# Gate groups between the stages of the first mixer, and one scheduling round in place of two

## The chip, the cores and the metric

The kernel runs on one core of a Trainium2 chip. The metric is the device time of one execution in microseconds; of several runs the median is taken.

## What is computed

Two transformer blocks are applied to 256 tokens of width 1024, in float32. The first block is a mixer of three branches (latent attention with 8 heads, a state-space branch with 32 groups, and cross attention to 256 memory tokens) and a gated feed-forward with a causal convolution. The second block has two layers, each a SwiGLU feed-forward, a mixer with three other branches and another SwiGLU feed-forward. For the first mixer the reference reads, cut to what matters here:

```python
h = rmsnorm(x, norm_mix_g)
c_q, c_kv, k_r, u_ssm, x_q, gate_logits = split_combined(h @ w_in)
y_a = mla_branch(c_q, c_kv, k_r, cos, sin, ...) @ w_o_mla
y_b = s5_branch(u_ssm, ...) @ w_o_ssm
y_c = cross_branch(x_q, mem, ...) @ w_o_cross
gates = sigmoid(gate_logits + b_gate).reshape(bsz, l, 3, D_MODEL)
merged = gates[:, :, 0] * y_a + gates[:, :, 1] * y_b + gates[:, :, 2] * y_c
x = x + merged @ w_out
```

## The kernel before

**Products.** Every large product is made of three: each operand is kept as a rounded high part (type fp32r) and the rest. `weights` (L452) loads weights in pieces of 512 KB into one of 5 buffers named raw, and `split` (L541) makes of each 128x512 half a high part wh (a cast on ScalarE) and a low part wl (a subtraction on VectorE). `proj` (L649) gives rows of tokens, in matmuls of up to 512 columns (PSUM tile pr); `proj_T` (L670) gives the transposed result for 256 weight columns in 48 matmuls of 256 columns (PSUM tile pt). Activations are brought into transposed, split form h by `norm_T` (L591): a square with a sum on ScalarE, a power on GpSimd, a scaling on VectorE (tile xs), transposes on TensorE and a split.

**The first mixer** (`mixer1`, L1305) normalises x, makes the latents (cq, ckv), the state-space input u and the cross queries xq, normalises the memory, and then works through the list `ORDER` (L30, loop L1375). Its letters: s0 and s1 are the halves of the state-space branch (`ssm_half`, L1045, with 16 small transfers that regroup u, maps built by `ssm_maps`, L981, of which the tiles xB are transposed into bT; products se of u with bT, a kT product, a scan on VectorE, and the products yb); h0 and h1 are groups of four attention heads (`heads`, L1365, and `mla_heads`, L1234: two projections of the latents, head norms, transposes qt, scores ms, softmax p, outputs mo); k0 and k1 are the two 512-column projections of the normalised memory (tile km); x0 is the cross attention (`cross_attn`, L1153, products cs and co); g0, g1 and g2 are the gate groups of the three branches (`gate_proj`, L816: four calls of `proj_T` and eight tanh on ScalarE into tiles named gate); b0 and b2 multiply the attention and the cross branch's output product with their gate (`branch`, L832). Behind the loop come the state-space GELU and GLU, the third branch and the output product (`merge_out`, L686).

**The rest of the program** (`two_block_kernel`, L1570) is a feed-forward and then two layers of feed-forward, mixer and feed-forward; `norm_x` (L637) stands ahead of each of these seven.

**The order of issue.** No engine instruction is issued while the program above runs. Each is recorded as an operation with an engine, an estimated cost, and the operations that it must follow (`Program.add`, L115). At the end a list scheduler orders all of them, for all engines and for the whole kernel. A round has two passes. `backward` (L154) schedules from the end and takes among the operations that are ready the one that stands latest in the order it was given; the time it gives to an operation is its priority. `forward` (L198) then runs a model of the engines, and takes on each engine the ready operation with the smallest priority for which there is room. Room for a tile is counted against the base order: an operation that stands later than the first one still open gets new tiles only if the base order, followed from there, still finds room for all its own.

```python
if pos[i] > lo:
    v = live[tag]
    ...
    bad = v[lo:pos[i]].max() > self.caps[tag]
```

The caps are 65 work tiles, of which 34 may be split weights, 5 raw buffers, 8 h tiles and 8 PSUM banks. `plan` (L350) begins with the program order as base, and each further round takes the order that the round before gave as its base. `issue` (L358) asks for two rounds and issues the operations in the order that the second gave. Each engine then runs its own instructions in that order and waits where an operand is not there yet.

Of the kernel before, what the change touches and what calls it, by code (L numbers as in the profile page):

```python
# [26 lines left out]
AHEAD = 500  # L27
MARGIN = 0.0
SLOW = 1.0
ORDER = "s0 h0 k0 k1 x0 h1 s1 g0 g1 g2 b0 b2"  # L30
STEPS = [1, 2, 3, 4] + [4 * q for q in range(1, 9)] + [32 * p for p in range(8)]
MAGIC = 12582912.0
TWO_PI = 6.2831850
# [41 lines left out]
class Program:  # L75
# [279 lines left out]
            order = self.forward(prio, order)[1]  # L355
        return order

    def issue(self, tc, rounds=2):  # L358
        with tc.manual_schedule():
            for i in self.plan(rounds):  # L360
                self.ops[i].call()
# [44 lines left out]
class Ctx:  # L406
# [898 lines left out]
    def mixer1(self):  # L1305
# [68 lines left out]
        kvm, y_mla, gates, y_cross = [], {}, {}, None  # L1374
        for step in ORDER.split():  # L1375
            q = int(step[1:])
# [293 lines left out]
```

## Time and profile before

| | us |
|---|---|
| median of 3 runs | 1574.74 |
| lowest and highest run | 1571.79, 1578.25 |
| the profiled execution | 1573.03 |
| its span, first to last instruction | 1571.3 |
| TensorE busy with matmuls | 1553.6 |
| TensorE busy with weight loads | 1430.9 |
| VectorE busy | 1025.7 |
| ScalarE busy | 840.1 |
| GpSimd busy | 101.7 |

A matmul's busy time runs from its start to a modelled end, and matmuls overlap in the pipeline; so a mean duration is longer than the distance between two starts, and a short wait can hide in the overlap. PE is TensorE's matmuls, PEld its weight loads, DVE VectorE, ACT ScalarE, POOL GpSimd and SP the engine whose queue issues the transfers. A wait is named by the instruction that waited and by what released it. L398 and L497 are helpers that issue nearly everything, so instructions are told apart by the names of their tiles.

### The profile page before, as it was taken

Reading aid. Unit: us, or ns where it says so; the run is one execution under the profiler, and the core shown is the slowest. Engines: PE = TensorE matmul, PEld = TensorE weight load, DVE = VectorE, ACT = ScalarE, POOL = GpSimd, SP = SyncE. Lnnn points to the kernel's source line nnn. Section 1 sums busy time; section 2 is a strip of 40 time slices with the busy share of each in tenths; the row PEclk is TensorE's granted clock in tenths of the full one; section 3 lists DMA queues with packets and bytes.
Section 4 is the critical chain, followed back from the end, with each engine's and each line's share of the span. In section 5 each row is a group of like instructions: output and inputs, shape, how many; then the busy total and the mean of one; then the engine's idle time right before and its main releaser. Section 6 shows DMA issues by size and latency. Waiting matters only on the chain.

```text
span 1571.3 us, 28497 instructions
## 1 busy us (share of the span) xinstructions
PE 1553.6 (99%) x11145; PEld 1430.9 (91%) x11145; DVE 1025.7 (65%) x1820; ACT 840.1 (53%) x1759; POOL 101.7 (6%) x204
## 2 busy tenths in 40 slices
PE   9999999999999999999999999999999999999998
PEld 7889999899989999889998999899998899989997
DVE  7896897787676545756657554665457656575543
ACT  8766665765555544555446444455345554464442
POOL 5114600000000000000000000000000000000000
PEclk9999999999999999999999999999999999999999
DMA  8556164566556656555647665466664556476650
GB/s 284 174 151 178 44 211 138 191 217 212 185 175 221 208 195 210 158 158 164 212 138 235 200 208 193 148 221 203 207 209 148 167 162 198 146 233 209 203 186 28
DMA packets 214230, 287.79 MB, mean 183 GB/s; under 512 B 13904, under 2 KB 170192, under 8 KB 214096
## 3 DMA queue, kind: packets, MB, share of 16 engines
q1 hardware_dynamic: 213952, 285.71, 57.0%
q8 instruction: 88, 1.44, 0.4%
q14 instruction: 46, 0.38, 0.1%
q10 hardware_dynamic: 144, 0.26, 0.0%
HBM read 284.36 MB, written 1.05 MB: 182 GB/s over the span
## 4 chain that ended last, share of the span: by engine, by line
PE 89%; DVE 4%; ACT 2%; DMA 2%; issue 1%; POOL 0%; POOLq 0%; DVEq 0%; ACTq 0%
PE pt L497 50%; PE acc L497 21%; PE pr L497 7%; PE up L497 4%; PE tr L522 2%; ACT wh L398 1%; DVE wl L398 1%; DMA raw<-in_w_ffn_dram 1%; DVE xs L398 1%; DMA raw<-in_w_in_dram 1%; DVE x L398 1%; PE se L497 1%; PE ms L497 0%; PE warm L629 0%; PE yb L497 0%
## 5 line engine op out<-in xcount | busy, mean ns | idle before, releaser
L398 DVE TENSOR_TENSOR wl<-raw,wh 128x512 fp32r<-128x512 f32 x1045 | 657.2, 686 | 193.9 <-ACT wh L398 184.0
L497 PE MATMUL pt<-h,wh 128*128 128x256 f32 x4224 | 736.1, 277 | 0.0
L398 ACT CAST wh<-raw 128x512 fp32r<-128x512 f32 x1045 | 578.3, 618 | 147.2 <-DMA raw<-in_w_in_dram 43.3
L497 PEld LDWEIGHTS pt<-h,wh 128*128 128x128 f32 x4224 | 642.4, 188 | 2.8 <-issue 0.2
L497 PE MATMUL pt<-h,wl 128*128 128x256 f32 x2112 | 584.1, 277 | 0.0
L497 PEld LDWEIGHTS pt<-h,wl 128*128 128x128 f32 x2112 | 397.0, 188 | 0.7 <-issue 0.5
L497 PE MATMUL acc<-wh,gh 128*128 128x512 f32 x440 | 170.6, 388 | 0.0
L497 PE MATMUL acc<-wh,gl 128*128 128x512 f32 x440 | 170.6, 388 | 0.0
L497 PE MATMUL acc<-wl,gh 128*128 128x512 f32 x440 | 170.4, 387 | 0.0
L497 PE MATMUL pr<-wh,h 128*128 128x512 f32 (+2 forms) x480 | 130.8, 355 | 2.4 <-DVE h L398 2.3
L398 ACT CAST gh<-sg 128x512 fp32r<-128x512 f32 x47 | 29.2, 621 | 147.5 <-DVE sg L398 147.5
L497 PE MATMUL up<-wh,h 128*128 128x512 f32 x320 | 100.8, 390 | 0.1
L497 PEld LDWEIGHTS pr<-wh,h 128*128 128x128 f32 x480 | 84.5, 188 | 16.0 <-DVE h L398 2.5
L497 PEld LDWEIGHTS acc<-wh,gl 128*128 128x128 f32 x440 | 82.6, 188 | 17.0
L497 PEld LDWEIGHTS acc<-wl,gh 128*128 128x128 f32 x440 | 82.5, 188 | 16.0
L497 PEld LDWEIGHTS acc<-wh,gh 128*128 128x128 f32 x440 | 82.6, 188 | 15.9
L398 DVE TENSOR_TENSOR sg<-sg,pt 128x512 f32<-128x512 f32 x36 | 24.8, 688 | 110.1 <-PE pt L497 110.1
L398 ACT ACTIVATE sg<-pt 128x512 f32<-128x512 f32 x36 | 21.5, 598 | 130.4 <-PE pt L497 130.4
L497 PE MATMUL pr<-wl,h 128*128 128x512 f32 (+2 forms) x240 | 85.0, 354 | 0.0
L398 POOL TENSOR_TENSOR rs<-s,mhalf 128x1 f32<-128x1 f32 x20 | 16.4, 820 | 961.8 <-DVE s L398 961.8
L497 PEld LDWEIGHTS up<-wh,h 128*128 128x128 f32 x320 | 59.7, 188 | 12.5 <-ACT h L398 0.6
L398 ACT ACTIVATE junk<-x 128x512 f32<-128x512 f32 x36 | 22.7, 631 | 79.1 <-DVE x L398 76.2
(352 smaller groups left out, 1639.8 us busy)
## 6 DMA issues: line engine op xcount, KB each, us to landing
raw<-in_w_ffn_dram SPq DMA_DIRECT2D x264, 512.0 KB, 5.0
raw<-in_w_in_dram SPq DMA_DIRECT2D x124, 512.0 KB, 5.0
raw<-in_w_up_dram SPq DMA_DIRECT2D x44, 512.0 KB, 4.8
raw<-in_w_out_dram SPq DMA_DIRECT2D x24, 512.0 KB, 4.8
raw<-in_w_down_dram SPq DMA_DIRECT2D x22, 512.0 KB, 4.5
raw<-in_w_mem_kv_dram SPq DMA_DIRECT2D x8, 512.0 KB, 4.5
raw<-in_w_branch_ret_dram SPq DMA_DIRECT2D x8, 512.0 KB, 3.5
raw<-in_w_o_mla_dram SPq DMA_DIRECT2D x4, 512.0 KB, 3.5
```

Source lines behind the costliest of these rows:

```text
L398: self.prog.add(self.name, lambda: getattr(self.eng, op)(**kw), self.cost(op, kw), list(aps.values()), writes, "fast" if self.name == "dve ...
L497: self.prog.add("pe", lambda: self.nc.tensor.matmul(ps, lhsT=lhsT, rhs=rhs, start=start, stop=stop), ns, [lhsT, rhs], [ps])
L522: self.prog.add("pe", lambda: self.nc.tensor.transpose(out, src, ident), 109, [src, ident], [out])
```

## The change

Two lines. The gate groups g0 and g1 move forward in the list, the memory projections, the cross attention and their order against h1 and s1 change with it, and the scheduler makes one round, so that the program order is the base for the whole kernel.

```diff
-ORDER = "s0 h0 k0 k1 x0 h1 s1 g0 g1 g2 b0 b2"
+ORDER = "s0 g0 h0 h1 g1 s1 k0 k1 x0 g2 b0 b2"
...
-    def issue(self, tc, rounds=2):
+    def issue(self, tc, rounds=1):
         with tc.manual_schedule():
             for i in self.plan(rounds):
                 self.ops[i].call()
```

## Rows read from the trace of the kernel before

**Rows 1.** The page, busy time of each engine over the whole span.

```profile
span 1571.3 us, 28497 instructions
PE 1553.6 (99%) x11145; PEld 1430.9 (91%) x11145; DVE 1025.7 (65%) x1820; ACT 840.1 (53%) x1759; POOL 101.7 (6%) x204
```

**Rows 2.** Busy time by stretch: length, engines' busy us and counts, clock, DMA.

```profile
0.00:256.00 256.00, 246.24 (x2084) 225.99 (x2085) 213.74 (x437) 177.84 (x471) 78.73 (x164) 0.99 0.56 171
256.00:1571.00 1315.00, 1307.32 (x9063) 1204.86 (x9061) 811.98 (x1384) 662.27 (x1288) 23.00 (x40) 1.00 0.58 186
```

**Rows 3.** TensorE's waits, 0 to 256 us: total us, times, longest.

```profile
PE pr L497 <- DVE h L398: 2.3, 1, 2.3
PE tr L522 <- DVE ckv L398: 1.4, 1, 1.4
PE tr L522 <- DVE p L398: 1.3, 1, 1.3
...
PE yb L497 <- DVE sg L398: 0.9, 1, 0.9
PE se L497 <- ACT bT L398: 0.8, 1, 0.8
PE mo L497 <- ACT p L398: 0.7, 1, 0.7
...
PE tr L522 <- POOL x L392: 0.3, 1, 0.3
PE tr L522 <- DVE xB L398: 0.3, 1, 0.3
```

**Rows 4.** TensorE's waits, 256 us to the end.

```profile
PE tr L522 <- DVE xs L398: 0.7, 4, 0.2
PE tr L522 <- DVE sg L398: 0.3, 1, 0.3
```

**Rows 5.** Busy time by stretch around the slow stretch, in the columns of rows 2.

```profile
157.00:162.00 5.00, 3.64 (x29) 2.86 (x28) 4.18 (x14) 3.83 (x10) 3.43 (x10) 1.00 0.32 105
162.00:170.00 8.00, 8.00 (x61) 7.41 (x62) 6.43 (x14) 3.45 (x7) 4.85 (x9) 0.59 0.22 66
```

**Rows 6.** Instructions of the gate tiles: ns shortest/median/longest, first and last start.

```profile
L398 ACT ACTIVATE gate<-pt,hbg x24: 457/470/505, 106.9 to 219.0; 128x256 f32<-128x256 f32 x24
```

**Rows 7.** TensorE in order of time, s0's and s1's transposes: start, us, idle before.

```profile
93.56 0.60 PE L522 MATMUL tr<-par,xB 128*128 128x128 f32 x4
93.91 0.48 PE L497 MATMUL pt<-h,wh 128*128 128x256 f32 x2
...
158.20 1.14 PE L522 MATMUL tr<-par,xB 128*128 128x128 f32 x8
159.60 0.63 PE L522 MATMUL tr<-par,xB 128*128 128x128 f32 x4 [0.26 <-POOL x L392]
160.48 0.63 PE L522 MATMUL tr<-par,xB 128*128 128x128 f32 x4 [0.25 <-DVE xB L398]
161.96 5.73 PE L497 MATMUL se<-u,bT 128*128 128x64 f32 x32 [0.85 <-ACT bT L398]
```

**Rows 8.** The chain that ended last, state-space products of s0: start, us.

```profile
97.06 1.75 PE se L497 x16
```

**Rows 9.** What SP's queue waited for: total us, times, longest.

```profile
SPq L449 <- DVE wl L398: 1169.7, 494, 11.6
```

**Rows 10.** Transfers by name: count, KB each, median us to landing.

```profile
raw<-in_w_in_dram SPq DMA_DIRECT2D x124, 512.0 KB, 5.0
```

**Rows 11.** TensorE in order of time around 463 us, the up products between left out.

```profile
463.07 0.49 PE L497 MATMUL up<-wh,h 128*128 128x512 f32 x1
...
467.38 1.06 PE L522 MATMUL tr<-par,xs 128*128 128x128 f32 x8 [0.18 <-DVE xs L398]
```

**Rows 12.** Busy time by stretch, 256-column and mostly 512-column products, columns of rows 2.

```profile
720.00:808.00 88.00, 88.00 (x768) 88.00 (x768) 53.71 (x89) 43.72 (x82) 0.00 (x0) 1.00 0.63 200
...
564.00:575.00 11.00, 11.00 (x51) 9.13 (x50) 9.38 (x16) 7.07 (x13) 1.40 (x6) 1.00 0.52 172
```

## The prediction

> **What bounds the kernel now.** I read the page's busy times first, then the busy time on either side of the end of the first mixer, then what TensorE waited for on either side, and last the places where it waited. TensorE has matmuls in flight for 1553.6 us of a span of 1571.3 us [rows 1], so 17.7 us of idle time is all that shows. Of it, 256.00 - 246.24 = 9.76 us lie in the first 256 us, the first mixer, and 1315.00 - 1307.32 = 7.68 us in everything behind it [rows 2]. The lists of waits say what that time is. In the mixer they are 2.3 us for the normalised memory on its way to the key and value product, 1.4 us for a latent, 1.3 and 0.7 us for softmax rows, 0.9 us for the state-space products, 1.4 us (0.8 + 0.3 + 0.3) for the second half's matrices [rows 3]; the rest of the 9.8 us, 1.8 us, is the start's, ahead of any stage that moves. Behind the mixer TensorE waits for other engines 1.0 us in all [rows 4]; the rest there is sequencer time and the store at the end, in which no product is left to run. The clock adds one loss that idle time doesn't show: it was at 2.4 GHz nearly throughout, but the stretch 162 to 170 us has a mean grant of 0.59, that is, most of it at 1.2 GHz; just before it, from 157 to 162 us, TensorE was busy 3.64 of 5.00 us [rows 5].
>
> So an order of instructions is the whole subject. The work stays what it is: no matmul, cast, subtraction or transfer is added or dropped, the sum of the durations is the same, and what can move is some 10 us of waits and one slow stretch in the mixer, and whatever a different schedule does to the 1315 us behind it.
>
> **The change, part by part.** The profiled execution took 1573.03 us, 1.7 us over its span and 1.7 us under the median of 1574.74 us; the sum is made on 1573.0 and 1.7 us is added for the median.
>
> *The order of the stages in the program.* Groups g0 and g1 (4 products of 48 matmuls each, 8 transfers of 512 KB, 16 casts and 16 subtractions a group) come forward, g0 to just behind the state-space half s0, g1 to just ahead of s1; k0, k1 and x0 (8 transfers, 16 casts and subtractions, the cross attention) go back behind s1, and the two head groups h0 and h1 stand together. The program order isn't the order of issue: already now a gate's tanh runs at 106.9 us and the last at 219.0 us, though the groups stand at the end of the list [rows 6], so gate products already serve as filler. What I cost is what the named waits become.
>
> (a) k0 moves behind both head groups and s1, so the normalised memory is wanted tens of us later than now, when TensorE stood 2.3 us for it [rows 3]. Taken: -2.3 us. Bounds: -2.3, or 0 where another late tile takes its place (the nearest row is the 1.4 us for a latent).
>
> (b) The latents are made ahead of the list, and VectorE, which makes them, is as full as before (213.74 of 256 us [rows 2]). The 1.4 us stay: 0.
>
> (c) s0 stays first, with gate products behind it before (by the schedule) and after (by the program): its 0.9 us stay. Bounds: -0.9 to +0.9.
>
> (d) The softmax waits, 1.3 + 0.7 us, came from one head group. Two of them stand together now, each with the same chain from scores over exponentials to transposes; gate products on both sides are filler, but in the profile they were there too. Taken: 0. Bounds: -2.0 to +2.0.
>
> (e) s1's preparation. In the profile 16 transposes of its matrices run from 158.20 us with nothing between them and gaps of 0.26, 0.25 and 0.85 us [rows 7]; s0's same transposes have gate products between them, and no wait. With g1 written just ahead of s1, s0 is the nearer row. Taken: -1.4 us. Bounds: -1.4 to +1.4.
>
> (f) The slow stretch follows (e). By the chain 32 state products took 5.73 us in it, where 16 took 1.75 us for s0 [rows 7, 8]: 5.73 - 2 x 1.75 = 2.2 us more, and that is the least, since a head group's and the kT products stand in the stretch too. By the grant, 8.00 us at 0.59 did what 4.7 us would at 2.4 GHz: 3.3 us [rows 5]. Taken: -3.3 us, for the whole stretch, since (e) goes with it. Bounds: -3.3, or +3.3 where the changed order makes one such stretch more than now.
>
> What moves with the stages on other queues: SP's transfers wait for freed buffers, 494 times for the subtraction that frees one [rows 9], so k0's and g0's weights only change places in that queue, and TensorE never waited for a transfer by name [rows 3, 4]. The second half's 16 small transfers pass ahead of k0's weights; its memsets and the head groups' rotations change places on GpSimd, which is idle 256.00 - 78.73 = 177.27 us of the mixer [rows 2]. Cost 0; if that cover went, a late 512 KB weight would cost part of its 5.0 us from issue to landing [rows 10].
>
> *One round in place of two.* The second round takes the first one's order as its base: for ties, for the priorities and for which tiles may be taken early. Without it the base is the program order, over the whole kernel. No row shows such a schedule. From below: behind the mixer only 1.0 us of waits is there to be won [rows 4]. From above: there are seven normalisations ahead of a feed-forward or mixer, each covered by products of the other token tile. At the one near 463 us, up products begin at 463.07 us and cover the second tile until its transposes at 467.38 us; without cover that is 4.3 us [rows 11], 30 us for seven. I take +2.8 us, 0.4 us each: the row nearest is the wait of 0.18 us there, which says that cover is just enough now and little is needed to miss. As a bound I keep half the cover, +15 us.
>
> The sum: -2.3 - 1.4 - 3.3 + 2.8 = -4.2 us, 1568.8 us, with 1.7 us **1570.5 us**, a quarter of a per cent under the median. The ends: -2.3 - 0.9 - 2.0 - 1.4 - 3.3 - 1.0 = -10.9 us, 1563.8 us; and 0.9 + 2.0 + 1.4 + 3.3 + 15 = +22.6 us, 1597.3 us.
>
> **How much room is there?** The rows say some 10 us of waits and 3.3 us of clock. The Trainium skill, "Perfetto Trace Analysis", section "Identifying the Most-Contended Engine", holds matmul busy time for a bad measure and judges headroom by the busy share of weight loads. By that share, 91%, 140.4 us would be open [rows 1], and a better order could win far more than my sum. The trace bears it out little: where 256-column products run back to back weight loads are busy 88.00 of 88.00 us, but where mostly 512-column ones do, TensorE has no gap and the loads are busy 9.13 of 11.00 us [rows 12]. The share falls with the shape there, not with a stall.
>
> **The rivals.** A difference under 0.5% (7.9 us) is about what a measurement of this kernel can't tell from no change.
>
> *All of it goes.* Gate products between the stages cover every chain: the waits of the mixer but the 1.8 us at its start (9.8 - 1.8 = 8.0 us) and the 3.3 us of clock, and the single round costs nothing: 1573.0 - 11.3 + 1.7 = 1563.4 us. For it: six of the eight waits of the mixer's stages stand in s0, s1 and the head groups, which the gate groups now flank. Against: gate products were at hand during most of them, and TensorE waited because an instruction placed ahead of them was late. By the Trainium skill's measure up to 140.4 us could go, to 1434 us; the rows above leave that 0.01 of this rival's chance.
>
> *The order issued hardly differs.* Gates were spread from 106.9 to 219.0 us already [rows 6], and the scheduler may undo the rearrangement: 1574.7 us, give or take 3 us. Against it: k0's place is bound to its program position through the tie-break.
>
> *The single round loses cover behind the mixer.* With the program order as base, the next stage's weights and tiles are taken later, because the program order's own peaks hold the room. Its place is the seven normalisations. At 2.5 us each it costs 17.5 us; with -7.0 us from the mixer the time is 1573.0 + 10.5 + 1.7 = 1585.2 us. It decides from (7.9 + 7.0) / 7 = 2.1 us each. For it: the cover is tight (0.18 us of wait). Against: the cover follows from the program order itself, in which the second tile's last products stand behind the first tile's.
>
> **How the numbers follow.** The forecast has 0.32, the unmoved order 0.15; both are within 0.5%, so 0.47. The full gain has 0.28, all of it faster by over 0.5%. The lost cover, with its like in the mixer, has 0.25, slower by over 0.5%. The range reaches from 1562 us, the full gain and the ends of its scatter, to 1587 us, just past the lost cover; about 0.1 is left out on each side. The middle cases alone lie between 1567 and 1582 us.
>
> **What would show it.** Right: no wait of the key and value product for the memory; the second half's transposes with gate products between them; the grant 1.00 through the mixer; the merge of the mixer starting 6 to 8 us sooner; behind it the same stretches as now, longer by under 0.5 us at each normalisation. Wrong: waits for softmax rows or state products that total over 10 us, a second slow stretch, or waits of 2 us and more ahead of the up products.

## The result, and the profile after

| | before | after |
|---|---|---|
| median, us | 1574.13 | 1583.2 |
| lowest and highest run | 1571.07, 1578.25 | 1581.15, 1585.06 |
| the profiled execution | 1573.03 | 1585.06 |
| its span | 1571.3 | 1583.3 |
| its mean granted clock | 0.997 | 0.993 |

The changed kernel is slower: the ratio over five runs of each is 1.0062, with a 95% interval of 1.0045 to 1.0079, that is 9.1 us. It lies in the predicted range and on the other side of the forecast. The profiled execution of the kernel after is the slowest of its five, that of the kernel before is a little under its median; so the two profiles differ by more, 12.0 us, than the medians. The page of the kernel after, where [rows 1] stood before:

```profile
span 1583.3 us, 28503 instructions
PE 1560.4 (99%) x11145; PEld 1436.5 (91%) x11145; DVE 1024.6 (65%) x1820; ACT 840.6 (53%) x1759; POOL 96.7 (6%) x204
```

The work is the same, x11145 matmuls, and TensorE is busy 6.8 us longer with it, which a wait cannot do and a slower clock can. Next the busy time by stretch, cut where the mixer's output product (tile acc) has just begun, at 260.29 us; the columns are those of [rows 2]. The kernel before, cut at the same product (255.67 us), follows:

```profile
0.00:260.29 260.29, 250.27 (x2082) 229.07 (x2083) 209.41 (x432) 176.51 (x467) 73.88 (x164) 0.97 0.53 164
260.29:1583.30 1323.01, 1310.12 (x9064) 1207.47 (x9063) 815.15 (x1389) 664.07 (x1293) 22.78 (x40) 1.00 0.58 185
```

```profile
0.00:255.67 255.67, 245.91 (x2082) 225.74 (x2083) 213.41 (x437) 177.76 (x471) 78.73 (x164) 0.99 0.56 171
255.67:1571.30 1315.63, 1307.65 (x9064) 1205.12 (x9063) 812.31 (x1384) 662.34 (x1289) 23.00 (x40) 1.00 0.58 185
```

So 4.6 us were lost in the mixer, after as many matmuls (x2082), and 7.4 us behind it. Idle time in the mixer is 260.29 - 250.27 = 10.0 us, where it was 9.8 us; the grant fell from 0.99 to 0.97. Behind it idle time rose from 8.0 to 12.9 us.

TensorE's waits after the change, first those up to 275 us ([rows 3] before), in total us, times, longest:

```profile
PE tr L522 <- DVE xB L398: 4.3, 1, 4.3
PE warm L629 <- DVE warm L392: 1.3, 1, 1.3
PE kT L497 <- POOL cT L392: 1.2, 1, 1.2
PE pr L497 <- ACT h L398: 1.1, 1, 1.1
PE pr L497 <- DVE wl L398: 1.1, 2, 0.8
```

Then those behind it ([rows 4] before):

```profile
PE up L497 <- ACT h L398: 4.8, 5, 2.3
PE ss L497 <- ACT qks L398: 1.5, 1, 1.5
```

Every wait of the mixer's stages that the prediction named has gone: the memory, the latent, the softmax rows, the products yb and se. Others stand in their place, one of 4.3 us for tile xB among them; and behind the mixer up products wait for the split activations h. The clock is read from four short stretches, in the columns of [rows 5]:

```profile
11.00:15.00 4.00, 3.69 (x15) 3.33 (x15) 4.00 (x10) 4.00 (x11) 1.05 (x3) 0.57 1.10 355
79.00:83.00 4.00, 3.10 (x16) 2.95 (x17) 3.79 (x11) 1.17 (x2) 1.48 (x6) 0.57 0.03 10
181.00:192.00 11.00, 10.34 (x59) 7.99 (x60) 6.96 (x14) 2.55 (x7) 7.92 (x14) 0.53 0.01 3
840.00:844.00 4.00, 4.00 (x13) 3.11 (x12) 3.42 (x8) 2.55 (x6) 0.94 (x1) 0.57 0.44 125
```

TensorE ran at 1.2 GHz for some 3.4 us from 11 us, 3.4 us from 79.3 us, 10.2 us from 181.7 us and 3.4 us from 840.5 us, 20.4 us together, where the kernel before had some 6.8 us [rows 5]; since 1.2 GHz is half of 2.4, the slow time of a stretch is twice its length times what the grant lacks of 1, as in 2 x 4.00 x (1 - 0.57) = 3.4 us. The 13.6 us more at half the clock cost 6.8 us, which is what TensorE's busy time grew by. Each of the four stretches follows a wait of TensorE: 1.13 us for h that end at 9.50 us, the 4.30 us for xB, 2.30 us for h that end at 839.34 us, and ahead of the longest stretch this one:

```profile
181.66 0.65 PE L497 MATMUL kT<-cT,x 128*32 128x128 f32 x8 [1.18 <-POOL cT L392]
```

That leaves three theories, with the letters used below. **C**, SP's queue: under the new list the second half's small transfers are issued much too early and hold up the weights of the head group behind them. **G**, the clock: chains of transposes and short products now stand where the clock falls. **A**, the single round: cover is lost behind the mixer. A rival to C and G is that the new list is no worse in itself, and that the single round alone costs the time.

### The profile page after: what moved, and what is told of

It reads as the page before. It is cut to its first block, busy times and chain, and to the rows that moved or that the text cites. A ratio compares the mean times of both kernels' runs of the same rounds, so it can differ in the third digit from the quotient of the medians.

```text
span 1583.3 us, 28503 instructions
## 1 busy us (share of the span) xinstructions
PE 1560.4 (99%) x11145; PEld 1436.5 (91%) x11145; DVE 1024.6 (65%) x1820; ACT 840.6 (53%) x1759; POOL 96.7 (6%) x204
## 4 chain that ended last, share of the span: by engine, by line
PE 92%; DVE 3%; DMA 2%; issue 1%; ACT 1%; SPq 0%; POOL 0%; POOLq 0%; DVEq 0%; ACTq 0%
PE pt L497 49%; PE acc L497 20%; PE pr L497 9%; PE up L497 7%; PE tr L522 2%; DVE wl L398 1%; DMA raw<-in_w_in_dram 1%; DMA raw<-in_w_ffn_dram 1%; PE ms L497 0%; SPq L449 0%; PE yb L497 0%; DVE x L398 0%; ACT wh L398 0%; PE glu L497 0%; DMA raw<-in_w_up_dram 0%
```

## The experiments

**The list and the round apart.** e1 keeps the old list and makes one round; e2 takes the new list and makes two.

```diff
(e1, on the kernel before)
-    def issue(self, tc, rounds=2):
+    def issue(self, tc, rounds=1):
(e2, on the kernel after)
-    def issue(self, tc, rounds=1):
+    def issue(self, tc, rounds=2):
```

> The old list with one round. Theory A (the single round is what costs behind the mixer, since it issues the first token tile's transposes and its cast of h later): behind the mixer the same 6 to 8 us as in the changed kernel appear, with waits of up products for the cast of h of some 4 to 5 us in all; the mixer is within 3 us of the kernel before; the time is 1578 to 1583 us. Rival B (the list is what costs, in the mixer and through what it shifts): 1572 to 1576 us, waits of up products under 1 us.

> The new list with two rounds. Theory A: behind the mixer as in the kernel before, no wait of up products over 0.5 us; what is left of the loss is the mixer's, at most 5 us: 1572 to 1579 us. Rival B: the mixer loses its 4 to 5 us and some of the waits behind it stay: 1579 to 1584 us.

Measured, in medians (with the ratio to the kernel before, and its interval):

| | two rounds | one round |
|---|---|---|
| old list | 1574.3 | 1592.9 (1.0124, 1.0108 to 1.0140) |
| new list | 1581.2 (1.0051, 1.0038 to 1.0065) | 1583.2 (1.0062, 1.0045 to 1.0079) |

The new list alone costs 7 us, so the rival falls. e1 lies above both of its expected ranges. A single round costs 18.6 us with the old list and 2.0 us with the new one (these two intervals overlap, so the 2.0 us may be nothing): the two edits don't add. TensorE's waits of e1 in its first 275 us say where:

```profile
PE se L497 <- ACT bT L398: 4.5, 1, 4.5
PE pr L497 <- ACT h L398: 4.4, 2, 3.3
PE yb L497 <- DVE sg L398: 2.9, 1, 2.9
```

These are chains of the mixer, and e1's output product begins only at 272.5 us. TensorE's idle time up to there is 272.50 - 254.03 = 18.5 us, where the kernel before had 9.8 us, and 10.1 us behind it (8.0 us). The clock of e1's runs was 0.9915 on average, that of the kernel before beside them 0.9971; (0.9971 - 0.9915) x 1593 = 8.9 us is an estimate of what that cost, about half of the loss. The gates' tanh run from 130.4 us on in e1, from 106.9 us in the kernel before [rows 6] and from 71.8 us in the kernel after. So it may be that with the old list as base the gate products come too late to cover the chains, and that the new list makes the single round bearable there; no run shows it. e2 has nearly the wait of after:

```profile
PE tr L522 <- DVE xB L398: 4.1, 1, 4.1
PE ms L497 <- ACT qkT L398: 2.2, 1, 2.2
```

So the wait for xB belongs to the list and not to the round.

**What the wait for xB hangs on.** It is followed back in the kernel after. TensorE in order of time (start, us, idle before and its releaser in brackets):

```profile
75.21 0.38 PE L497 MATMUL pr<-wl,ckvh 128*128 128x512 f32 x1
...
79.89 1.09 PE L522 MATMUL tr<-par,xB 128*128 128x128 f32 x4 [4.30 <-DVE xB L398]
```

VectorE, which makes xB, had been idle earlier, and ScalarE ahead of it; first ScalarE's, then VectorE's row:

```profile
67.12 0.51 ACT L398 CAST wh<-raw 128x384 fp32r<-128x384 f32 x1 [1.25 <-DMA raw<-in_w_q_b_dram]
```

```profile
67.67 0.56 DVE L398 TENSOR_TENSOR wl<-raw,wh 128x384 fp32r<-128x384 f32 x1 [3.97 <-ACT wh L398]
```

The transfer that came last is a head group's weights. SP issued it here, in order of time:

```profile
51.26 3.66 SPq L449 DMA_DIRECT2D u<-uT  x5
55.02 0.53 SPq L449 DMA_DIRECT2D raw<-in_w_in_dram  x1
55.61 1.89 SPq L449 DMA_DIRECT2D u<-uT  x2
57.60 0.53 SPq L449 DMA_DIRECT2D raw<-in_w_q_b_dram  x1
58.17 6.21 SPq L449 DMA_DIRECT2D u<-uT  x9
64.48 0.53 SPq L449 DMA_DIRECT2D raw<-in_w_q_b_dram  x1
```

The 16 small transfers u<-uT are the second half's, not wanted until some 175 us; before the change they were issued from 85 to 97 us. Together they fill SP for 3.66 + 1.89 + 6.21 = 11.8 us, with the head group's pieces of w_q_b between and behind them. The piece issued at 64.48 us, 192 KB, is the one for which ScalarE and then VectorE stood.

e3 takes these 16 transfers out of the issued order and puts them back behind the head groups' last weights. Only SP's order changes.

```diff
-            for i in self.plan(rounds):
+            for i in self.late(self.plan(rounds)):
                 self.ops[i].call()
...
+    def late(self, order):
+        move = set([i for i, op in enumerate(self.ops) if op.kind == "move"][16:])
+        order = [i for i in order if i not in move]
+        at = order.index(self.behind) + 1
+        return order[:at] + sorted(move) + order[at:]
```

> The changed kernel with the 16 small transfers of the second state-space half issued behind the head groups' weights, where SP is free, and every other engine's order untouched. Theory C (those transfers, 0.6 us each on SP, hold up the weights of the head groups, VectorE waits for these, and the first half's matrices and TensorE's 4.3 us wait follow): the wait at 80 us falls under 1.5 us, and the slow stretch that followed it goes; the time is 4 to 6 us under the changed kernel, 1577 to 1580 us. Rival D (VectorE is full there anyway, and its order sets the wait): 0 to 1 us under it, 1582 to 1584 us.

e4 undoes one step that theory A suspected behind the mixer. At 839.34 us of the kernel after, up products wait 2.30 us for h; the transposes of the first token tile stand behind all output products, and ScalarE's cast of h stands behind a cast of weights that was itself late:

```profile
838.18 0.62 ACT L398 CAST wh<-raw 128x512 fp32r<-128x512 f32 x1 [1.96 <-DMA raw<-in_w_ffn_dram]
838.71 0.58 ACT L398 CAST h<-tr 128x512 fp32r<-128x512 f32 x1
```

At the same place the kernel before has the first tile's transposes between output products, and its cast of h ahead of that cast of wh. e4 moves them so at all seven normalisations, in TensorE's and ScalarE's order:

```diff
+    def hoisted(self, order):
+        for b, trs, cast in self.hoist:
+            move = [*trs, cast]
+            pe = [i for i in order if self.ops[i].eng == "pe"]
+            before = pe[pe.index(trs[0]) - (7, 4)[b]]
...
+            order = order[:at] + move + order[at:]
```

> The changed kernel with the first token tile's transposes at each of the seven normalisations of x issued 7 and 4 products earlier, and their casts of h right behind them, as in the kernel before; all else untouched. Theory A: the waits of up products for the cast of h (4.8 us) fall under 1 us and the slow stretch near 840 us goes: 4 to 6 us under the changed kernel, 1577 to 1580 us. Rival E (the weights are what is late, and TensorE then waits for the low part of a weight instead): under 1.5 us won, 1581.5 to 1584 us.

Measured: e3 1578.01 us (1.0031, 1.0019 to 1.0043), 5.2 us under the kernel after; e4 1585.8 us (1.0084, 1.0067 to 1.0100), 2.6 us over it, with intervals that overlap, and outside both of its expected ranges. TensorE's wait for xB in e3, whose lines stand 6 further down, and then SP's order in it:

```profile
PE tr L528 <- DVE xB L404: 2.2, 1, 2.2
```

```profile
67.79 0.37 SPq L455 DMA_DIRECT2D raw<-in_w_kv_b_dram  x1
68.21 10.18 SPq L455 DMA_DIRECT2D u<-uT  x16
```

With nothing changed but the place of 16 transfers in one queue, the time falls and the wait halves: C holds for the time. Two things that it expected didn't come: the wait was to fall under 1.5 us, and the slow stretch behind it was to go. VectorE begins with xB at 74.85 us rather than 78.90 us; but it is busy 9.72 of the 10.00 us from 70 to 80 us, so the 2.2 us that are left look like its own order. And in e3's profile the slow stretch behind the wait is longer, not shorter (below); that run, 1581.89 us, is one of the slowest of e3's twelve. e4's waits behind the mixer:

```profile
PE tr L533 <- DVE xs L409: 5.9, 9, 1.1
PE ss L508 <- ACT qks L409: 1.6, 1, 1.6
```

The up products' wait has gone and the transposes' wait for xs, which the kernel after doesn't have there, is 5.9 us at nine places: the wait has moved one instruction on. So the place of those transposes and casts by itself isn't what the single round costs; that reading of A fell, and A itself stayed open.

**C without the round, and the clock.** e5 is e2 with e3's edit. For G, three kernels put extra products among the transposes of both state-space halves: ahead of the first and third of each group of four stands one product of 256 columns in bf16, whose result the transposes overwrite; 16 products in all. e6 does so on the kernel before, e7 on e3.

```diff
-        bT = [[self.copied(self.transposes(m), "bT") for m in part] for part in xin]
+        bT = [[self.copied(self.busy_transposes(m), "bT") for m in part] for part in xin]
...
+    def busy_transposes(self, src):
+        i = len(self.prog.ops)
+        ps = self.transposes(src)
+        for op in self.prog.ops[i:i + 4:2]:
+            op.call = lambda call=op.call: (self.fill(ps), call())
+        return ps
+
+    def fill(self, ps):
+        rhs = self.ident.bitcast(BF16)
+        self.nc.tensor.matmul(ps[:, 256:512], lhsT=self.identb, rhs=rhs, start=True, stop=True)
```

For A, e8 keeps the single round's times for the operations of the first mixer and takes two rounds' times for all the rest:

```diff
+    def merged(self):
...
+        for r in range(2):
...
+            starts.append(start)
+        n = self.border
+        shift = max(starts[0][:n]) - max(starts[1][:n])
+        key = [starts[0][i] if i < n else starts[1][i] + shift for i in range(len(self.ops))]
```

> The new list with two rounds, and the 16 small transfers of the second state-space half issued behind the head groups' weights, all else untouched. Theory C (these transfers on SP are the list's cost): 3 to 5 us under the same kernel without it, 1576 to 1578 us, and the 4.1 us wait for the first half's matrices falls under 2 us. Rival F (the list costs through the head groups' softmax and projections, whose waits sum to 6 us there): within 1.5 us of 1581 us.

> The kernel before, with 8 extra bf16 products of 256 columns among the transposes of each state-space half's matrices, into a bank that those transposes overwrite; 16 products in all, about 0.1 us each. Theory G (the clock falls because TensorE does little but transposes with gaps there): the slow stretch of 6.8 us goes or shortens, the mean granted clock of the runs rises by 0.001 to 0.002, and the time is 0 to 3 us under the kernel before, 1571 to 1574 us. Rival H (the clock falls for another reason, or at a random time): the products only cost, 0.5 to 2 us more, 1574.5 to 1576.5 us, clock as before.

> The changed kernel with the second half's transfers late, as before, and with the same 16 extra products. Theory G: the slow stretches after 77 us and after 182 us shorten (13.7 and 6.8 us in the profile without the products), the mean clock rises by 0.002 to 0.004, 2 to 5 us under the same kernel without them, 1573 to 1576 us. Rival H: 1578 to 1580 us.

> The changed kernel, but the operations behind the first mixer in the order that a second round gives them; the mixer keeps the order of the first round. Theory A (the single round costs 6 us behind the mixer): the waits of up products and of the stick-breaking scores (6.3 us) fall under 2 us, 4 to 6 us under the changed kernel, 1577 to 1579.5 us. Rival I (the loss behind the mixer comes from where the mixer ends and what is loaded ahead then, not from the order behind it): 1581.5 to 1584 us.

Measured:

| | median, us | ratio to before | mean clock of its runs |
|---|---|---|---|
| before | 1573.58 | | 0.997 |
| e5 | 1574.99 | 1.0011 (0.9999 to 1.0022) | 0.998 |
| e6 | 1572.43 | 0.9990 (0.9979 to 1.0000) | 0.998 |
| e7 | 1574.23 | 1.0005 (0.9996 to 1.0014) | 0.998 |
| e8 | 1578.79 | 1.0034 (1.0020 to 1.0048) | 0.994 |

e5 is 6.2 us under e2: C is worth as much with two rounds as with one, and it is nearly all that the new list costs there. The mean clock rose with it, from 0.9948 to 0.9976, which by (0.9976 - 0.9948) x 1581 = 4.4 us is most of the 6.2 us; so what the late weights cost came for a good part as clock, and C and G are not separate there.

e7 is 3.8 us under e3, with 16 products more. Two stretches of e3 by clock, and then the same two of e7, in the columns of [rows 5]:

```profile
77.00:91.00 14.00, 13.86 (x89) 13.01 (x88) 9.17 (x26) 9.13 (x34) 6.87 (x15) 0.52 0.28 81
181.00:192.00 11.00, 9.82 (x68) 7.75 (x68) 8.06 (x16) 2.48 (x8) 7.97 (x15) 0.69 0.01 2
```

```profile
77.00:91.00 14.00, 13.60 (x133) 12.57 (x132) 13.20 (x31) 11.54 (x40) 6.58 (x15) 1.00 0.29 83
181.00:192.00 11.00, 10.79 (x95) 9.74 (x96) 8.31 (x18) 6.60 (x24) 3.94 (x6) 1.00 0.01 4
```

The grant is 1.00 where it was 0.52 and 0.69, and in the same 14 us 133 matmuls run in place of 89. e3's profile shows one of its slowest runs, but over all runs the mean clock is 0.9947 in e3 and 0.9984 in e7, and their intervals are apart: G holds for this list. The wait for xB ahead of the first stretch is 2.2 us in e7 as in e3, so the wait alone doesn't decide; that for cT ahead of the second one fell from 1.2 to 0.5 us. What the products do is shorten the slow stretch: e9 below has the same mixer, wait and products as e7, and in its profile the clock does fall behind the wait, but for 3.4 us (a grant of 0.57 from 77 to 81 us, 1.00 from 181 to 192 us), where e3 has 13.7 us. On the kernel before the same edit shows little; e6's slow stretch is still there, with a grant of 0.66:

```profile
162.00:170.00 8.00, 7.34 (x60) 6.62 (x60) 7.12 (x17) 3.66 (x8) 5.66 (x10) 0.66 0.21 68
```

Its 1.2 us of gain have an interval that touches 1.0000: not settled.

e8 is 4.4 us under the kernel after, and in its profile 1316.0 us follow the output product's start, as in the kernel before (1315.6 us; 1323.0 us in the kernel after), with 8.0 us of idle time where the kernel after has 12.9 us. The profiles differ there by more than 4.4 us, since that of e8 is of its quickest run and that of the kernel after of its slowest. TensorE's only wait behind the mixer is

```profile
PE tr L545 <- DVE xs L421: 1.3, 5, 0.4
```

where after has 4.8 + 1.5 = 6.3 us. So the single round's loss under the new list lies behind the mixer, as A says, and two rounds' order there takes it back. Which of that order's many differences does it isn't shown; the one that was tried, in e4, is not it.

**All three together.** e9 is e8 with e3's and e7's edits; e10 is e5 with e7's.

> The changed kernel with all three remedies: the second half's transfers late, the 16 extra products among the transposes, and the operations behind the mixer in the order of a second round. If the three losses are separate (theories C, G and A), their gains add up: 1583.2 - 5 - 4 - 4.5, about 1569 to 1571 us, 3 to 4 us under the kernel before, with the mixer's output product starting near 252 us as without the second round. Rival J (they share one loss, so that one remedy hides another): 1573 to 1576 us.

> The new list with two rounds, the second half's transfers late and the 16 extra products: what the list is worth without the single round. Theory: as the kernel with late transfers alone (1575.0 us) less what the clock gives back, at most 2 us: 1572.5 to 1575 us, so the list with two rounds is no better than the old list with the extra products (1572.4 us). Rival J: 1570 us or less.

e9 took 1570.51 us (0.9979, 0.9971 to 0.9988), 3.1 us under the kernel before; e10 1574.44 us (1.0004, 0.9993 to 1.0016). The three steps before were 5.2 us (e3), 3.8 us (e7, on top of e3) and 4.4 us (e8), 13.4 us in all, which would give 1569.8 us; they nearly add. e9's waits in the mixer, and its first 252.8 us by the columns of [rows 2]:

```profile
PE tr L551 <- DVE xB L427: 2.2, 1, 2.2
PE warm L669 <- DVE warm L421: 1.3, 1, 1.3
PE pr L526 <- ACT h L427: 1.2, 1, 1.2
```

```profile
0.00:252.80 252.80, 246.44 (x2098) 225.69 (x2099) 208.97 (x433) 176.41 (x468) 74.70 (x164) 0.99 0.54 170
```

Its output product begins at 252.8 us, 2.9 us sooner than in the kernel before, with 16 matmuls more and idle time of 252.80 - 246.44 = 6.4 us where that had 9.8 us [rows 2]. With two rounds for the mixer too, e10 gets to 255.7 us, no sooner than the kernel before. The fair comparison for the 16 products is e6, the kernel before with the same ones: there the output product begins at 256.2 us, with 9.7 us of idle time. So in these profiles the new list does cover the mixer's chains better, and with the first round's order only; in the change as it was made this stood under three losses. In time e9 is 1.9 us under e6, with intervals that overlap (0.9971 to 0.9988 and 0.9979 to 1.0000): that the change gains anything without its losses isn't settled.

## Why the prediction was wrong

The forecast, 1570.5 us, is e9's time by chance: e9 moves 16 transfers, adds 16 products and takes two rounds behind the mixer, none of which the forecast had. Two of the three signs of being wrong that the prediction named came: a second slow stretch, and a wait of 2 us and more ahead of the up products. Point by point:

- **(a), (d), (e), the named waits: gone, as forecast or better.** No wait of [rows 3] that the prediction dealt with is left, also those for the latent and the softmax rows that (b) and (d) kept at 0. The forecast's error is what took their place: idle time in the mixer is 10.0 us, where 9.8 - 3.7 = 6.1 us was forecast. For (e) the number is luck: 14 of the second half's 16 transposes stand in a row at 176.85 us, with no gate products between them, and a wait came behind them, the 1.18 us for cT.
- **"What moves with the stages on other queues: cost 0" failed.** The prediction named the 16 small transfers that "pass ahead of k0's weights" and the price of a late 512 KB weight, and then argued from TensorE's waits that no transfer was late. In the new list they stand ahead of a head group's weights, and each takes SP's sequencer about 0.59 us. By e3 that cost 5.2 us, by e5 6.2 us, the clock that went with it included. TensorE's waits still name no transfer; they name xB, some steps down the chain. The Trainium skill, "DMA: Bandwidth & Descriptors", section "Issuing engines are not separate DMA queues", holds that what an issuing engine's sequencer spends on a transfer is usually small beside the transfer. The rows show a case that this doesn't cover: one such transfer of 16 KB takes SP some 0.6 us, with 1.8 us from issue to landing (medians), 9 of them in a row took SP 6.21 us, and what counted was the 192 KB of weights behind them. The same step priced GpSimd by its idle time, 177.27 us; but it is GpSimd's last clearing of cT, up to 181.6 us, for which TensorE stood 1.18 us ahead of the longest slow stretch. No run moves that clearing, so its price stays open.
- **(f), the clock, had the wrong sign.** It was taken at -3.3 us because (e) would go. (e)'s waits did go, and the slow stretch stayed: from 181.7 us, in the second half's products, right behind the wait for cT that took their place. Waits go ahead of all four slow stretches, but a wait alone doesn't set how long one lasts: behind the same 2.2 us for xB the clock stayed low for 13.7 us in e3, for 3.4 us in e9 and not at all in e7, the last two with 16 products more. What else decides stays open. The bound "one such stretch more" was too small too: three more came, at 11, 79 and 840 us, the last one behind the 2.30 us wait of the up products. The mean clock was 0.9938 in the five runs of the kernel after and 0.9969 in the 30 runs of the kernel before beside e5 to e8; (1 - 0.9938) x 1583 - (1 - 0.9969) x 1574 = 4.9 us is an estimate of the cost, about half of the 9.1 us, and the fill of e7 takes back 3.8 us. With -3.3 us in the sum, this term is the furthest off.
- **The single round: the right sign and place, under-sized.** Taken at +2.8 us, 0.4 us for each of seven normalisations; e8 measures 4.4 us behind the mixer. The mechanism was near: TensorE's waits of 4.8 us fall on the up products, at five of the seven normalisations. What the prediction had not seen is that the round's cost depends on the list, 18.6 us with the old one and 2.0 us or nothing with the new.
- **The rival with the lost cover** came out near in time, 1585.2 us against 1583.2, and half right: its place is where part of the loss was, but at 0.6 us (4.4 / 7) a normalisation, far from the 2.1 us from which it was to decide. The rest came from C and G, for which there was no rival on the slow side.

Put together, by the two profiles: the forecast had -3.7 us of waits in the mixer, +2.8 us of waits behind it and -3.3 us of clock. TensorE's idle time shows +0.2 us in the mixer and +4.9 us behind it (12.9 - 8.0), and the slow stretches +6.8 us: 11.9 us, against 12.0 us between the two spans. The medians are 9.1 us apart, with some 4.9 us for the clock. The gains of e3, e7 and e8 are another cut through the same loss and can't be put into this sum one by one: e3 and e5 gave back waits and clock together.

## What to carry to other kernels

When stages change places, write down for each queue, SP's too, which transfers now stand ahead of which, and when each is wanted; a string of cheap transfers that is wanted late should be issued late, and its delay shows not as a wait for a transfer but as an idle helper engine some steps up the chain. Waits that vanish are replaced by the next ones in line, so count a gain only once the instruction behind is known to be ready. Read the granted clock of each short stretch before and after an edit: a schedule can lose as much there as in waits, with TensorE busy throughout.

## What the runs showed of the hardware

The granted clock wasn't steady from run to run of the same kernel: of all runs of the kernel before beside these experiments the quickest took 1569.63 us at a mean grant of 0.999 and the longest 1578.77 us at 0.995; by (0.999 - 0.995) x 1574 = 6.3 us, an estimate, most of its scatter of 9.1 us is the clock's. The clock fell behind a wait of 2.2 us and stayed at 1.2 GHz for some 13 us in a stretch that itself had no gap to speak of but held transposes and narrow products (e3, 77 to 91 us: TensorE busy 13.86 of 14.00 us, grant 0.52). Behind a wait as long, with products that compute nothing among the transposes (16 in all), it stayed at 2.4 GHz in the profile of e7 and fell for 3.4 us in that of e9, so that adding work made the kernel 3.8 us faster (e7 against e3). The stretch at 11 us came in the profile of after and not in that of before (its grant there was 1.00). e3, whose order differs from that of after only by transfers issued much later, has a grant of 1.00 there, and a wait for h of 0.46 us in place of 1.13 us; so the order of instructions alone doesn't bring it, and its cause stays open.
